# Hybrid encoder layer: the sums of w_out are prepared in the first chunk instead of the second, the parts of the first products move beside P, and the second chunk's conv is drained one unit later

## The chip, the cores and the metric

The kernel runs on one core of a Trainium2 chip. The metric is the device time of one execution in microseconds (us); the times of a kernel are given as the median of several runs.

## The reference, cut to what matters

One encoder layer over 18 blocks of 128 tokens (two of a prompt, sixteen of a sample) and 16 learned meta tokens. One projection feeds a windowed attention with 8 query and 2 key heads and a depthwise convolution of width 31; both are gated, joined and projected out.

```python
h = rmsnorm(z, norm_w)
q, k, v, g_att, c_val, c_glu, g_conv = split(h @ w_in)
q, k = rmsnorm(q, q_norm_w), rmsnorm(k, k_norm_w)          # per head, 64 wide
att = windowed_gqa(q, k, v, sink) * silu(g_att)            # 128 back, 128 ahead, meta keys, sink
u = c_val * sigmoid(c_glu)
y = depthwise_conv(u, conv_w) + conv_b                     # 31 taps
cnv = silu(layernorm(y, ln_w, ln_b)) * silu(g_conv)
out = z + concat(att, cnv) @ w_out
```

## The kernel before, in words

All products are in fp32r, each operand split in a high part and the rest of it, and each product made in three passes (high by high, high by low, low by high). A tile's high part is a cast on ScalarE (ACT), its low part a subtraction on VectorE (DVE).

**Projection.** The tokens form six groups (group 0 has 400 columns with the meta tokens, the others 384), three of them a chunk. For each chunk the units of w_in (256 columns each) are run through in a fixed order: the four conv units U_C (value and glu of 128 channels), the conv gates U_GC, the attention gates U_GA, k and v (U_KV), and the two query units U_Q. A product of a unit with a group or a block of 128 tokens is a tile pj in PSUM, 24 matmuls (8 slices of the model width in three passes). There are four such tiles, so a product has to wait until the product four ahead of it was read. L1028 is the product whose result has tokens in rows (q, k, v), L1012 the other. For q the reader is DVE: L1159 multiplies pj by rqq, the inverse root mean square that GpSimd (POOL) makes from ACT's squares (L177, L178). For k and v they are L1186 and L1178, and L1196 to L1199 transpose and scale k.

**Conv.** It runs on DVE, 31 taps for each of four channel groups and each chunk (L1086 for the first tap, L1095 for the other 30), on 1167 columns at once. The taps wait in a queue conv_q; each part of the program that has other work calls tick with the time that TensorE (PE) will spend on it, and tick issues taps for so much time. owe takes off the time of other DVE work. A loop "while conv_q: tick(3000)" stands ahead of one unit of each chunk and issues all taps that are left.

**LayerNorm of the conv.** For each block of 128 tokens, ln_block issues three steps, a tick apart: s1 transposes the four channel groups (lnt, PE, L250) and takes the statistics (DVE L253, L254, then POOL for the inverse root and the scaled mean); s2 applies them (zn, DVE L263); s3 transposes back (lnu, PE, L269), ACT makes the silu (L272) and the result is stored. One block is begun in a tick, from LN_WAIT ticks on after the chunk's last tap was issued.

**Attention and the output.** Attention begins inside the second chunk's last query unit: spread is called there after each product and begins the slots of attention, n counting the calls. After the projection attention_rest runs the other slots, with PE and POOL in program order. slot_step issues what is due in a slot t: acts (loads, gates, splits), the scores S of a block, and jobs, the output products. Two blocks b0 = 2p and b1 = 2p + 1 make a pair p. The first two 128-row slices of each half of w_out are multiplied in a form with seven products of sums instead of eight; their names are c1, s3, s2, s1, t0, t1, s4, and JOBS gives each the slot, counted from 16 p, in which product (L719, tile yb) issues it. An operand of activations lies in HOME, the place of a tile rest in which parts finds the high and the low half; two_parts (L677, L678) fills it. rest takes the space of the projection's weights, so it exists from attention_rest on, and with_rest puts off what needs it.

**The sums.** The seven operands of w_out, for two slices i, are made on the chip: presplit_sums loads four pieces of w_out (wor) and then takes one step a tick: 14 operands in all get a cast (ACT, L392, tiles woc, wot, wos) and a subtraction (DVE, L393) and a store of 512 KB to wod in DRAM; between them stand 8 differences of pieces (DVE, L397). An operand lies in one of the two buffers of the tag xn, which the row statistics of the input use also; the pieces take the four buffers of the tag xt, which the loads of x use. In split_at presplit_sums(0) is called behind the second group of the second chunk's second conv unit and presplit_sums(1) behind the last group of its third.

PIECES_W lists the 22 pieces of wod in the order in which they are wanted. The first APART go to tiles of their own, the next to slots of wo, loaded by load_wo, and the last ones to rest.

Inside the manual parts the order of PE or POOL is the program's. Elsewhere a scheduler that models the engines picks the order of each engine's instructions from what the program has issued, so moving work on one engine moves others' too.

Of the kernel before, what the change touches and what calls it, by code (L numbers as in the profile page):

```python
# [18 lines left out]
P = 128  # L19
# [28 lines left out]
W0 = 3  # L48
LN_WAIT = (9, 2)
LTAGS = "dbdbd" + "dcdcddddd"  # L50
# [31 lines left out]
NS = 2  # L82
PIECES_W = [("c1", 0), ("c1", 1), ("s3", 0), ("s3", 1), ("s2", 0), ("s2", 1), (6, 0), (6, 1), (7, 0), (7, 1)]
PIECES_W += [("s1", 0), ("s1", 1), ("t0", 0), ("t0", 1), (2, 0), (2, 1), (3, 0), (3, 1)]
PIECES_W += [("s4", 0), ("s4", 1), ("t1", 0), ("t1", 1)]
APART = 3
JOBS = (
# [21 lines left out]
SUMS = ("c1", "s3", "s2", "s1", "t0", "t1", "s4")  # L109
HOME = {"c1": 0, "t1": 0, "s3": 1, ("c", 0): 1, "s4": 1, "s1": 2, "s2": 3, ("c", 1): 3, "t0": 4, ("t", 0): 5, ("t", 1): 5}  # L110
QP = 7
# [4 lines left out]
U_C = [0, 1, 2, 3]  # L116
# [12 lines left out]
def hymba_kernel(  # L129
# [287 lines left out]
    def load_apart(i):  # L417
        if i < 2:
            t = pool["b"].tile([P, D], F32R, tag=f"wa{i}", name=f"wa{i}", bufs=1)
        else:  # L420
            t = cst["pt" if i < APART else "rest"][:, 6:8].rearrange("p a n -> p (a n)")
        wo[PIECES_W[i]] = t
        nc.sync.dma_start(t.bitcast(F32), wod[i])
# [247 lines left out]
    def parts(name):  # L671
        t = cst["rest"][:, HOME[name]].rearrange("p (h e n) -> p h e n", h=2, n=P)
        return t[:, 0], t[:, 1]
# [77 lines left out]
    for p in range(NB // 2):  # L751
        b0, b1 = 2 * p, 2 * p + 1
        for rel, f in (
            (5, lambda b0=b0: load_mix(b0)),
            (6, lambda b1=b1: load_mix(b1)),
            (9, lambda p=p: load_x(p, (0, 1))),
            (11, lambda b1=b1: mix_conv(b1)),
            (12, lambda b0=b0: mix_conv(b0)),
            (13, lambda p=p: with_rest(lambda: mix_diff(p))),
            (12, lambda p=p: load_x(p, (1, 1))),  # L760
            (13, lambda b1=b1: with_rest(lambda: two_parts("c1", cnt[b1][:, 0:NS, :]))),
            (14, lambda: with_rest(lambda: two_parts("s3", temp(0)))),
            (17, lambda b0=b0: two_parts(("c", 0), cnt[b0][:, NS:4, :])),
            (17, lambda p=p: load_x(p, (0, 0))),
            (20, lambda b1=b1: two_parts(("c", 1), cnt[b1][:, NS:4, :])),
            (18, lambda p=p: load_x(p, (1, 0))),
            (18, lambda p=p: add_kept(p, (1, 1), 0)),
            (20, lambda p=p: add_kept(p, (0, 0), 1)),
            (21, lambda p=p: add_kept(p, (1, 0), 0)),
        ):  # L770
            acts.setdefault(16 * p + rel, []).append(f)
        for rel, name, es in JOBS:
            to = late_jobs if name == "s3" else jobs
            if p == LAST and name in ("t1", (1, 0)):
                for c0 in (0, 256):
                    to.setdefault(16 * p + rel, []).append((p, name, es, c0, 256))
            else:
                to.setdefault(16 * p + rel, []).append((p, name, es))
# [32 lines left out]
    def spread(b):  # L811
# [6 lines left out]
        if n == 9:  # L818
            mixing_open()
        if n in (10, 11, 12):  # L820
            load_apart(n - 10)
# [10 lines left out]
    def attention_rest():  # L832
# [6 lines left out]
        for k in range(6):  # L839
            later(2 + k, lambda k=k: load_wo(12 + k))  # L840
        later(9, lambda: load_apart(len(PIECES_W) - 1))
        while slots:
# [7 lines left out]
    if True:  # L850
# [483 lines left out]
        for n3 in range(3):  # L1334
# [8 lines left out]
            (1, U_C[0], CHUNKS[1][2]): lambda: presplit_wo(3),  # L1343
            (1, U_C[1], CHUNKS[1][1]): lambda: presplit_sums(0),
            (1, U_C[2], CHUNKS[1][2]): lambda: presplit_sums(1),
        }

        for i, (c, u, g) in enumerate(items):
            if (c, u) == (1, U_KV) and g == CHUNKS[c][0]:
                while conv_q[0] or conv_q[1]:  # L1350
                    tick(3000)
# [118 lines left out]
```

## Time and profile before

| | |
|---|---|
| median of 3 runs | 950.04 us (948.38 to 951.31) |
| the profiled execution | 948.39 us |
| its span, first to last instruction | 946.6 us |
| mean granted TensorE clock | 0.996 |

The profile is of one execution. Its parts: busy time of each engine; what each engine waited for; a timeline of its instructions with the wait ahead of each in brackets and what ended it; and windows, which give for a stretch the busy time of each engine (with its number of instructions in brackets), the mean granted clock of TensorE, the share of time that the DMA engines were busy, and GB/s. In every row names lose their numbers (lnu for lnu8), and L is the line of the kernel. A busy figure alone says little here: an engine that is late matters only when PE waits for it.

### The profile page before, as it was taken

The numbers are of one execution on the slowest core, as the hardware profiler recorded it, in microseconds if no ns is written. First come the engines' busy times: TensorE is split into PE (matmuls) and PEld (weight loads), VectorE is DVE, ScalarE is ACT, GpSimd is POOL, SyncE is SP. The second block draws the span as 40 slices with busy tenths as digits, with TensorE's granted clock in tenths as the row PEclk, the third lists the DMA queues.
The fourth block names the chain that finished last, engine by engine and source line by source line (L and its number), as shares of the span: only waits on it lengthen the run. The fifth ranks groups of instructions, "written<-read, shape, count | busy, mean of one in ns | idle before, by whom it ended". The sixth has DMA issues, their size and how long they took to land. (4 is left out here: it accounts for less than half of the span.)

```text
span 946.6 us, 16874 instructions
## 1 busy us (share of the span) xinstructions
PE 929.8 (98%) x5734; PEld 878.8 (93%) x5734; DVE 778.6 (82%) x1340; ACT 445.5 (47%) x1229; POOL 358.9 (38%) x553
## 2 busy tenths in 40 slices
PE   8999999999999999999999889999999999999998
PEld 8999999999999999999999889887888888888887
DVE  5579999997977889999996763688888888897884
ACT  7432022253458742011111354567676776776772
POOL 4310000282558300000001452677665465546644
PEclk9999999999999999999999999999999999999999
DMA  8584345685756587333333468997565665665421
GB/s 304 169 273 194 134 176 179 247 294 189 207 169 194 185 285 260 147 114 140 131 139 133 143 194 272 376 374 210 166 181 170 185 197 153 186 199 168 144 92 48
DMA packets 146342, 182.80 MB, mean 193 GB/s; under 512 B 40944, under 2 KB 106816, under 8 KB 146128
## 3 DMA queue, kind: packets, MB, share of 16 engines
q1 hardware_dynamic: 146256, 181.72, 58.7%
q8 instruction: 45, 0.74, 0.3%
q14 instruction: 41, 0.34, 0.1%
HBM read 115.83 MB, written 65.85 MB: 192 GB/s over the span
## 5 line engine op out<-in xcount | busy, mean ns | idle before, releaser
L1012 PE MATMUL pj<-xh,ws 128*128 128x384 f32 (+1 forms) x1536 | 395.9, 338 | 0.1
L1095 DVE SCALAR_TENSOR_TENSOR y<-us,cw,y 128x1167 f32<-128x1167 f32 x240 | 329.3, 1431 | 0.1
L1012 PEld LDWEIGHTS pj<-xh,ws 128*128 128x128 f32 x1536 | 280.1, 188 | 0.4 <-ACT xh L1260 0.4
L1012 PE MATMUL pj<-xl,ws 128*128 128x384 f32 (+1 forms) x768 | 260.9, 340 | 0.1
L719 PE MATMUL yb<-wo,rest 128*128 128x512 f32 (+1 forms) x717 | 190.8, 399 | 0.0
L1028 PE MATMUL pj<-ws,xh 128*128 128x256 f32 (+1 forms) x880 | 165.2, 285 | 0.2 <-DVE kn L1186 0.2
L719 PEld LDWEIGHTS yb<-wo,rest 128*128 128x128 f32 x717 | 125.9, 189 | 22.6 <-DVE rest L678 0.2
L1012 PEld LDWEIGHTS pj<-xl,ws 128*128 128x128 f32 x768 | 144.1, 188 | 0.5 <-DVE xl L950 0.4
L1028 PEld LDWEIGHTS pj<-ws,xh 128*128 128x128 f32 (+1 forms) x880 | 137.5, 188 | 1.1 <-issue 0.4
L1028 PE MATMUL pj<-ws,xl 128*128 128x256 f32 (+1 forms) x440 | 124.6, 283 | 0.0
L1120 ACT ACTIVATE go<-pj 128x384 f32<-128x384 f32 x48 | 23.5, 490 | 154.2 <-PE pj L1012 140.3
L534 ACT ACTIVATE sb<-sb,nm 128x304 f32<-128x304 f32 (+5 forms) x144 | 77.8, 541 | 32.4 <-DVE nm L522 30.4
L177 POOL TENSOR_SCALAR ssk<-ssk 128x2 f32<-128x2 f32 x18 | 10.5, 582 | 209.1 <-ACT sqk L1134 208.9
L522 DVE CUSTOM_DVE_ANT_0 sb<-S,bias,vec 128x304 f32<-128x304 f32 (+5 forms) x144 | 74.1, 515 | 16.7 <-PE S L464 15.8
L560 POOL TENSOR_SCALAR sb<-sb,es 128x304 f32<-128x304 f32 (+5 forms) x144 | 73.2, 526 | 38.3 <-PE pT_x L580 17.0
L1028 PEld LDWEIGHTS pj<-ws,xl 128*128 128x128 f32 (+1 forms) x440 | 83.0, 189 | 0.2
L177 POOL TENSOR_SCALAR ssq<-ssq 128x4 f32<-128x4 f32 (+2 forms) x55 | 27.0, 491 | 109.5 <-ACT xn L875 70.4
L464 PE MATMUL S<-kw,q 128*128 128x304 f32 (+5 forms) x288 | 63.3, 302 | 0.6 <-issue 0.5
L464 PEld LDWEIGHTS S<-kw,q 128*128 128x128 f32 x288 | 52.5, 188 | 11.2 <-ACT keptFalse L737 0.8
L642 POOL TENSOR_TENSOR at<-at,ga 128x256 f32<-128x256 f32 x36 | 26.7, 742 | 75.1 <-DVE at L636 75.1
L730 DVE TENSOR_TENSOR yo<-yb,yo 128x512 f32<-128x512 f32 (+1 forms) x55 | 37.1, 674 | 15.3 <-PE yb L719 15.1
L988 DVE TENSOR_TENSOR ws<-wraw,ws 128x512 fp32r<-128x512 f32 x50 | 34.8, 727 | 8.2 <-ACT ws L987 8.2
(156 smaller groups left out, 1368.0 us busy)
## 6 DMA issues: line engine op xcount, KB each, us to landing
wd<-ws SPq DMA_DIRECT2D x36, 512.0 KB, 5.9
ws<-wd SPq DMA_DIRECT2D x36, 512.0 KB, 5.9
wraw<-in_w_in SPq DMA_DIRECT2D x52, 256.0 KB, 5.8
xn<-in_z SPq DMA_DIRECT2D x18, 512.0 KB, 5.4
gd<-go SPq DMA_DIRECT2D x48, 192.0 KB, 1.9
yo<-in_z SPq DMA_DIRECT2D x36, 256.0 KB, 3.7
wo<-wod SPq DMA_DIRECT2D x18, 512.0 KB, 7.5
out_y<-yo SPq DMA_DIRECT2D x35, 256.0 KB, 2.4
```

The costliest lines, as they stand in the source:

```text
L177: nc.gpsimd.tensor_scalar(src, src, scale, eps, op0=ALU.mult, op1=ALU.add)
L464: r = f(*a, **k)
L522: nc.vector.tensor_tensor_reduce(out=sb[:, n, c0:c1], in0=ps[:, 0:w], in1=cst["bias"][:, kv, at + c0 : at + c1], scale=1.0, scalar=nsnk[:, ...
L534: nc.scalar.activation(sb[:, n, c0:c1], sb[:, n, c0:c1], AF.Exp, bias=nm[:, n : n + 1], scale=-1.0, accum_out=rs[:, n : n + 1],)
L560: nc.gpsimd.tensor_scalar(sb[:, k, a0:a1], sb[:, k, a0:a1], es[:, k : k + 1], 1.0, op0=ALU.mult, op1=ALU.mult)
L642: nc.gpsimd.tensor_tensor(at[:, pr, :], at[:, pr, :], gat[b][:, pr, :], op=ALU.mult)
L719: nc.tensor.matmul(ps[:, :n], x[mi][:, i, :], w[wi], start=((name, e) in OPENS and k == 0), stop=(done and e == es[-1] and k == 2), skip_g ...
L730: nc.vector.tensor_tensor(y, ps[:, :n], y, op=ALU.add)
L988: pinned(eng.tensor_tensor(lo, raw[q], hi, op=ALU.subtract), k < 2)
L1012: nc.tensor.matmul(ps[:, :n], ws[:, d, wi, P * half_i : P * half_i + P], x[xi][:, d, o : o + n], start=(k == 0), stop=(k == 3 * ND - 1),)
L1028: nc.tensor.matmul(ps[:rows, :UW], x[xi][:, d, o : o + rows], ws[:, d, wi, :], start=(k == 0), stop=(k == 3 * ND - 1),)
L1095: nc.vector.scalar_tensor_tensor(y[:, yo + o0 : yo + o1], u[:, o0 + k : o1 + k], cw[:, j, k : k + 1], y[:, yo + o0 : yo + o1], op0=ALU.mul ...
```

## The change

It has six parts.

1. presplit_sums(0) and (1) are called behind the last group of the first chunk's first attention-gate unit and behind the first group of its U_KV.
2. The loop that drains conv_q stands ahead of U_Q[0] (keys[-2]) instead of ahead of U_KV in the second chunk, and LN_WAIT of that chunk is 1 instead of 2.
3. The parts move: c1 and t1 share slot 6 and s3, ("c", 0) and s4 slot 7 of the tile pt (called ptiles in the profile), which exists before rest does; the others take four places of rest instead of six. c1's split no longer waits for rest.
4. APART is 2: the pieces 2 to 19 lie one slot of wo later each, and the last two in rest.
5. In each pair b1's conv rows and gates are loaded before b0's.
6. In pair 0, c1's split is at step 12 and its product at step 14, one earlier than in the other pairs.

```diff
-LN_WAIT = (9, 2)
+LN_WAIT = (9, 1)
...
-APART = 3
+APART = 2
...
-HOME = {"c1": 0, "t1": 0, "s3": 1, ("c", 0): 1, "s4": 1, "s1": 2, "s2": 3, ("c", 1): 3, "t0": 4, ("t", 0): 5, ("t", 1): 5}
+HOME = {"c1": ("pt", 6), "t1": ("pt", 6), "s3": ("pt", 7), ("c", 0): ("pt", 7), "s4": ("pt", 7)}
+HOME.update({"s1": ("rest", 0), "s2": ("rest", 1), ("c", 1): ("rest", 1), "t0": ("rest", 2)})
+HOME.update({("t", 0): ("rest", 3), ("t", 1): ("rest", 3)})
...
     def load_apart(i):
-        if i < 2:
+        if i < APART:
             t = pool["b"].tile([P, D], F32R, tag=f"wa{i}", name=f"wa{i}", bufs=1)
         else:
-            t = cst["pt" if i < APART else "rest"][:, 6:8].rearrange("p a n -> p (a n)")
+            k = 2 * (i - len(PIECES_W) + 4)
+            t = cst["rest"][:, k : k + 2].rearrange("p a n -> p (a n)")
...
-            (5, lambda b0=b0: load_mix(b0)),
-            (6, lambda b1=b1: load_mix(b1)),
+            (5, lambda b1=b1: load_mix(b1)),
+            (6, lambda b0=b0: load_mix(b0)),
...
-            (13, lambda b1=b1: with_rest(lambda: two_parts("c1", cnt[b1][:, 0:NS, :]))),
+            (13 - (p == 0), lambda b1=b1: two_parts("c1", cnt[b1][:, 0:NS, :])),
...
         for rel, name, es in JOBS:
             to = late_jobs if name == "s3" else jobs
+            rel -= p == 0 and name == "c1"
...
-            (1, U_C[1], CHUNKS[1][1]): lambda: presplit_sums(0),
-            (1, U_C[2], CHUNKS[1][2]): lambda: presplit_sums(1),
+            (0, U_GA[0], CHUNKS[0][2]): lambda: presplit_sums(0),
+            (0, U_KV, CHUNKS[0][0]): lambda: presplit_sums(1),
         }
 
         for i, (c, u, g) in enumerate(items):
-            if (c, u) == (1, U_KV) and g == CHUNKS[c][0]:
+            if (c, u) == keys[-2] and g == CHUNKS[c][0]:
                 while conv_q[0] or conv_q[1]:
                     tick(3000)
```

The instructions of PE, DVE and ACT keep their number and kind; their order moves at three places. In the rows, names carry their numbers, lines of the changed kernel are up to six higher than those before, and "x4" is four in a row.

The first is PE near the end of the second chunk's k and v. lnt8 and lnu8 are the two transposes of block 8's LayerNorm, zn8 is what DVE makes between them, pj133 the last product of U_KV and pj134 the first of U_Q[0]. Before:

```order
L1028 MATMUL pj133_5633<-ws1_8_4949,xh5_3484 128x256
L269 MATMUL lnu8_5345<-ident_72,zn8_5287 128x128 x4
L250 MATMUL lnt10_5393<-ident_72,y1_0_3769 128x128
L250 MATMUL lnt10_5393<-ident_72,y1_1_3974 128x128
L250 MATMUL lnt10_5393<-ident_72,y1_2_4327 128x128
L250 MATMUL lnt10_5393<-ident_72,y1_3_4724 128x128
L1196 MATMUL kt12_5409<-ident_72,kn12_5324 128x128
L250 MATMUL lnt11_5462<-ident_72,y1_0_3769 128x128
L250 MATMUL lnt11_5462<-ident_72,y1_1_3974 128x128
L250 MATMUL lnt11_5462<-ident_72,y1_2_4327 128x128
L250 MATMUL lnt11_5462<-ident_72,y1_3_4724 128x128
L269 MATMUL lnu9_5414<-ident_72,zn9_5355 128x128 x4
```

The same place in the changed kernel:

```order
L271 MATMUL lnu8_5525<-ident_72,zn8_5467 128x128 x4
L1034 MATMUL pj133_5537<-ws1_8_4949,xh5_3564 128x256
L1034 MATMUL pj133_5537<-ws1_8_4949,xl5_3565 128x256
L1034 MATMUL pj133_5537<-ws1_8_4949,xh5_3564 128x256 x2
L1034 MATMUL pj133_5537<-ws1_8_4949,xl5_3565 128x256
L1034 MATMUL pj133_5537<-ws1_8_4949,xh5_3564 128x256
L252 MATMUL lnt10_5573<-ident_72,y1_0_3849 128x128
L252 MATMUL lnt10_5573<-ident_72,y1_1_4043 128x128
L252 MATMUL lnt10_5573<-ident_72,y1_2_4346 128x128
L252 MATMUL lnt10_5573<-ident_72,y1_3_4724 128x128
L1034 MATMUL pj134_5611<-ws1_6_5140,xh3_3116 128x256
L1034 MATMUL pj134_5611<-ws1_6_5140,xl3_3117 128x256
```

Before, lnu8 stood at the end of pj133, 15 of its matmuls behind the last transpose of lnt8, and lnu9 behind it with only transposes between. In the changed order lnt8 stands whole behind pj131 and lnu8 18 matmuls into pj133; lnt9 stands behind pj132, lnu9 in pj134, and the later blocks follow one about every product: from lnt8 to lnu8 there are 42 projection matmuls, from lnt9 to lnu9 47, then 48 for block 10, 40 for block 11 and 61 for block 12. lnu17, the last, stands behind pj141.

The second place is DVE in the first chunk's first query unit. y0_2 and y0_3 are the conv's taps, qs0_2 reads the product pj61, and wor and wos belong to the sums. Before:

```order
L1095 SCALAR_TENSOR_TENSOR y0_2_1350<-us0_2_740,cw_80,y0_2_1350 128x1167
L1159 TENSOR_TENSOR qs0_1_2597<-pj60_2561,rqq0_1_2590 128x256
L1095 SCALAR_TENSOR_TENSOR y0_3_1524<-us0_3_956,cw_80,y0_3_1524 128x1167
L1159 TENSOR_TENSOR qs0_2_2638<-pj61_2599,rqq0_2_2630 128x256
L1095 SCALAR_TENSOR_TENSOR y0_2_1350<-us0_2_740,cw_80,y0_2_1350 128x1167
L1199 SCALAR_TENSOR_TENSOR ks7_2503<-kt7_2501,kscale_81,ks7_2503 128x128
L1095 SCALAR_TENSOR_TENSOR y0_3_1524<-us0_3_956,cw_80,y0_3_1524 128x1167
```

The changed kernel:

```order
L1101 SCALAR_TENSOR_TENSOR y0_2_1350<-us0_2_740,cw_80,y0_2_1350 128x1167
L399 TENSOR_TENSOR wor22_1_2264<-wor22_1_2264,wor11_1_2258 128x2x256
L1101 SCALAR_TENSOR_TENSOR y0_3_1524<-us0_3_956,cw_80,y0_3_1524 128x1167
L1165 TENSOR_TENSOR qs0_1_2676<-pj60_2636,rqq0_1_2665 128x256
L1101 SCALAR_TENSOR_TENSOR y0_2_1350<-us0_2_740,cw_80,y0_2_1350 128x1167
L399 TENSOR_TENSOR wor21_1_2260<-wor21_1_2260,wor22_1_2264 128x2x256
L1101 SCALAR_TENSOR_TENSOR y0_3_1524<-us0_3_956,cw_80,y0_3_1524 128x1167
L395 TENSOR_TENSOR wos3_1_2563<-wor12_1_2262,wos3_1_2563 128x512
L1101 SCALAR_TENSOR_TENSOR y0_2_1350<-us0_2_740,cw_80,y0_2_1350 128x1167
L395 TENSOR_TENSOR wos2_1_2622<-wor22_1_2264,wos2_1_2622 128x512
L1165 TENSOR_TENSOR qs0_2_2718<-pj61_2678,rqq0_2_2709 128x256
L1205 SCALAR_TENSOR_TENSOR ks7_2574<-kt7_2572,kscale_81,ks7_2574 128x128
```

Of the 22 operations of the sums five stand ahead of the first L988 of unit 6 in the changed order, sixteen between it and qs0_2, and one behind qs0_3; qs0_2 has two taps more ahead of it than before and eight row scalings of x (L921) less. The first and the last of the 22 are 96 rows apart; before it was 53. The second chunk's DVE order is without them, and its last tap stands ahead of ks9.

The third place is PE where the projection ends (pj151 is its last product) and the output products yb begin. S2_0_0 are the scores of block 2, which need q2_2, the transposed and split copy of what qT2 makes. Before:

```order
L1028 MATMUL pj151_6625<-ws1_7_5702,xh5_3484 128x256
L719 MATMUL yb0_6743<-wa0_6235,rest_6707 128x512 x3
L719 MATMUL yb0_6743<-wa1_6289,rest_6707 128x512 x3
L464 MATMUL S1_1_3_6751<-kw1_5950,q2_1_6352 128x176 x2
L580 MATMUL pT1_c_0_6768<-ident_72,sb2_5966 128x128 x4
L464 MATMUL S2_0_0_6776<-kw0_5949,q2_2_6725 128x176 x2
L719 MATMUL yb0_6743<-ptiles_6186,rest_6707 128x512 x3
L719 MATMUL yb0_6743<-wo0_6363,rest_6707 128x512 x3
L614 MATMUL O0_1_6691<-ptiles_6186,vm_78 128x512
```

The changed kernel:

```order
L1034 MATMUL pj151_6624<-ws1_7_5606,xh5_3564 128x256
L723 MATMUL yb0_6716<-wa0_6235,ptiles_6186 128x512 x3
L723 MATMUL yb0_6716<-wa1_6289,ptiles_6186 128x512 x3
L467 MATMUL S1_1_2_6724<-kw1_5868,q2_1_6351 128x208 x2
L467 MATMUL qT2_6727<-ident_72,q2_6443 128x128 x4
L467 MATMUL S1_1_3_6752<-kw1_5868,q2_1_6351 128x176 x2
L583 MATMUL pT1_c_0_6767<-ident_72,sb2_5884 128x128 x4
L467 MATMUL S2_0_0_6775<-kw0_5867,q2_2_6732 128x176 x2
L723 MATMUL yb0_6716<-wo0_6362,ptiles_6186 128x512 x6
```

yb0's first six matmuls take their operand from ptiles instead of rest. S1_1_2 and qT2, which stood ahead of pj151 before, now stand behind these six, and between qT2 and S2_0_0 there are only S1_1_3 and pT1_c_0.

More of the change, by code (lines that the diff above doesn't have):

```diff
@@ L671, in parts @@
     def parts(name):
-        t = cst["rest"][:, HOME[name]].rearrange("p (h e n) -> p h e n", h=2, n=P)
+        place, k = HOME[name]
+        t = cst[place][:, k].rearrange("p (h e n) -> p h e n", h=2, n=P)
         return t[:, 0], t[:, 1]
@@ L819, in spread @@
             mixing_open()
-        if n in (10, 11, 12):
+        if n in (10, 11):
             load_apart(n - 10)
@@ L840, in attention_rest @@
             later(2 + k, lambda k=k: load_wo(12 + k))
-        later(9, lambda: load_apart(len(PIECES_W) - 1))
+        for k in range(2):
+            later(8 + k, lambda k=k: load_apart(len(PIECES_W) - 2 + k))
         while slots:
```

## The prediction

> **What bounds the kernel now.** I read the page first. TensorE (PE) is busy all but all of the span, so only what makes PE wait, or run at a lower clock, can move the time; time taken off another engine counts where PE waits for it.
>
> ```profile
> span 946.6 us, 16874 instructions
> PE 929.8 (98%) x5734; PEld 878.8 (93%) x5734; DVE 778.6 (82%) x1340; ACT 445.5 (47%) x1229; POOL 358.9 (38%) x553
> ```
>
> Next the list of PE's waits (us in total, times, longest). It names all that is to be had near the change: the conv's LayerNorm (lnu and lnt behind zn) and one wait of an output product for its operand (yb behind rest).
>
> ```profile
> PE lnu L269 <- DVE zn L263: 6.2, 2, 3.4
> PE O L614 <- DVE ptiles L597: 1.6, 1, 1.6
> PE yb L719 <- ACT rest L677: 1.0, 1, 1.0
> PE lnt L250 <- DVE zn L263: 0.5, 1, 0.5
> ```
>
> The timeline puts them at places (start, duration, wait in brackets), and the windows show the granted clock around the two long ones (the last four columns are POOL, PEclk, DMA share and GB/s).
>
> ```profile
> 540.62 0.66 PE L269 MATMUL lnu<-ident,zn 128*128 128x128 f32 x4 [2.79 <-DVE zn L263]
> 568.49 1.06 PE L269 MATMUL lnu<-ident,zn 128*128 128x128 f32 x4 [3.39 <-DVE zn L263]
> 614.87 0.50 PE L614 MATMUL O<-ptiles,vc 128*128 128x512 f32 x1 [1.65 <-DVE ptiles L597]
> 620.50 1.69 PE L719 MATMUL yb<-wa,rest 128*128 128x512 f32 x6 [1.04 <-ACT rest L677]
> 538.00:546.00 8.00, 5.38 (x33) 5.24 (x34) 4.74 (x10) 4.08 (x14) 4.42 (x12) 0.79 0.85 300
> 566.00:574.00 8.00, 5.51 (x34) 5.54 (x35) 1.62 (x2) 3.11 (x10) 2.09 (x8) 0.79 0.90 308
> 610.00:620.00 10.00, 7.77 (x57) 6.68 (x55) 7.92 (x20) 6.96 (x21) 8.60 (x16) 1.00 1.02 349
> ```
>
> So the second chunk's LayerNorm costs 2.79 + 3.39 + 0.5 (lnt, in the list) of idle time, and 0.21 x 8 = 1.68 us of lost clock behind each long gap: 6.7 + 3.4 = **10.1 us**. The 1.65 us gap at 614.87 left the clock at 1.00.
>
> **LayerNorm of the second chunk: -10.1, with 1.0 left.** The gaps come from order: PE's program has lnu8 in pj133, some 15 products behind the last transpose of lnt8, and little other work ahead of lnu9. This is how the chain ran where PE waited longest (two blocks' statistics together, then POOL's scale, then zn):
>
> ```profile
> 563.83 1.30 DVE L253 BATCH_NORM_STATS2 bs<-lnt 128x6 f32<-128x512 f32 x2 [0.23 <-PE lnt L250]
> 567.54 0.81 DVE L263 TENSOR_SCALAR zn<-lnt,mv 128x512 f32<-128x512 f32 x1 [1.83 <-POOL mv L256]
> ```
>
> From 563.83 to lnu at 568.49 it is 4.7 us. A projection matmul takes 2.82/24 = 0.118 us (rows at 266.76 and 267.11 below: 0.35 for three). In the changed order lnt8 to lnu8 has 42 of them between (4.9 us), lnt9 to lnu9 47 (5.5), lnt10 to lnu10 48 (5.7), lnt11 to lnu11 40 (4.7), lnt12 to lnu12 61 (7.2). All cover 4.7, the shortest just so. I take the whole 10.1 back, less 1.0 for short waits at the shortest ones (an estimate: two of 0.5, like lnt's). The new order needs the conv done earlier, since lnt8 stands whole behind pj131. The last taps were issued here:
>
> ```profile
> 530.50 2.90 DVE L1095 SCALAR_TENSOR_TENSOR y<-us,cw,y 128x1167 f32<-128x1167 f32 x2
> 329.42 0.69 DVE L393 TENSOR_TENSOR woc<-wor,woc 128x512 fp32r<-128x512 f32 x1 [1.06 <-ACT woc L392]
> 336.68 0.69 DVE L393 TENSOR_TENSOR wot<-wor,wot 128x512 fp32r<-128x512 f32 x1 [3.62 <-ACT wot L392]
> 337.76 0.68 DVE L397 TENSOR_TENSOR wor<-wor,wor 128x512 f32<-128x512 f32 x1
> 338.36 0.88 DVE L1086 TENSOR_SCALAR y<-us,cw,vec 128x1167 f32<-128x1167 f32 x1
> 357.33 0.69 DVE L393 TENSOR_TENSOR wot<-wor,wot 128x512 fp32r<-128x512 f32 x1 [2.06 <-ACT wot L392]
> ```
>
> The sums leave that stretch: 14 L393 and 8 L397, each 0.60 start to start (337.76 to 338.36), 13.2 us, and DVE's waits for their casts, 1.06 + 3.62 + 2.06 = 6.7. VectorE (DVE) is then some 20 us less behind, and the taps, which ended at 533.4, end near 513 and what the first chunk loses. pj131 ends 48 products ahead of the wait at 540.62 - 2.79 = 537.8, near 532: over 14 us of cover.
>
> **The sums in the first chunk: +3.1, and 0.9 for their own waits.** DVE has little room there. From 219.95 to the last tap's end it is idle 56.15 - 52.42 = 3.7 us; just ahead of it is a wait of 4.07.
>
> ```profile
> 219.95:276.10 56.15, 55.90 (x472) 55.25 (x470) 52.42 (x80) 24.00 (x128) 28.93 (x40) 1.00 0.64 200
> 219.95 1.29 DVE L988 TENSOR_TENSOR ws<-wraw,ws 128x512 fp32r<-128x512 f32 x2 [4.07 <-ACT ws L987]
> 230.48 2.19 DVE L921 SCALAR_TENSOR_TENSOR xt<-xt,vec,bc 128x384 f32<-128x384 f32 x4 [0.67 <-PE bc L904]
> 262.81 0.42 DVE L1159 TENSOR_TENSOR qs<-pj,rqq 128x256 f32<-128x256 f32 x1
> 269.56 0.42 DVE L1159 TENSOR_TENSOR qs<-pj,rqq 128x256 f32<-128x256 f32 x1 [1.19 <-POOL rqq L178]
> 274.73 1.42 DVE L1095 SCALAR_TENSOR_TENSOR y<-us,cw,y 128x1167 f32<-128x1167 f32 x1
> 276.07 0.42 DVE L1159 TENSOR_TENSOR qs<-pj,rqq 128x256 f32<-128x256 f32 x1
> 266.76 0.28 PE L1028 MATMUL pj<-ws,xl 128*128 128x256 f32 x1
> 267.11 0.29 PE L1028 MATMUL pj<-ws,xl 128*128 128x256 f32 x1
> 283.66 0.38 PE L250 MATMUL lnt<-ident,y 128*128 128x128 f32 x2
> ```
>
> Five of the 22 operations stand ahead of 219.95 in the new order and fall into the 4.07. Sixteen of the others stand ahead of qs0_2, which empties pj61 for pj65, and two taps more (1.34 each, 274.73 to 276.07), less eight row scalings (L921, 2.19 for four with the last one's tail, so 0.53 each): 9.6 + 2.7 - 4.2 = 8.1, of which 2.4 fall into the waits that lie ahead of qs0_2 in the trace. So qs0_2 moves from 262.81 to 268.5 and ends at 268.9. PE wants pj65 at 283.66 - 6 x 2.82 = 266.7: a wait of 2.2. The same walk for the next two gives 0.4 and 0.5 more (pj66, pj67): **3.1**. The last tap then ends at 286.5, and the transposes behind pj70, at 283.66 + 3.1 = 286.8, find it done.
>
> That walk has DVE without a gap. Its bounds: 0 more, and 6.7 more if its waits for casts come along (the three rows above). I take 0.9, nearer the lower end: the 22 operations stand among 96 rows of DVE's order instead of 53, so each cast has more time, and DVE comes to qs later than before, when POOL's factors are long done. PE would wait for DVE one for one.
>
> [...]
>
> **The start of the output products: +1.3.** c1's parts no longer wait for rest, and yb's 1.04 goes. But S1_1_2 and qT2, which were ahead of pj151, now stand behind it, and S2_0_0 follows them closely. The chain from qT to its copy, at the next such place:
>
> ```profile
> 637.79 0.60 PE L464 MATMUL qT<-ident,q 128*128 128x128 f32 x4
> 638.15 0.71 PE L614 MATMUL O<-ptiles,vm 128*128 128x512 f32 x2
> 638.43 0.58 ACT L484 CAST q<-qT 64x512 fp32r<-64x512 f32 x1 [0.71 <-PE qT L464]
> 640.34 0.69 DVE L487 TENSOR_TENSOR q<-qT,q 64x512 fp32r<-64x512 f32 x1
> 622.03 0.36 PE L464 MATMUL S<-kw,q 128*128 128x176 f32 x2
> 622.58 0.44 PE L464 MATMUL S<-kw,q 128*128 128x176 f32 x2
> ```
>
> qT leaves PE at 638.15, and the copy is whole at 640.34 + 0.69 = 641.03: 2.9 us. Between qT2 and S2_0_0 there is only 622.58 - 622.03 = 0.55 of PE work (S1_1_3, pT1_c_0). PE waits 2.3 there, where it waited 1.04: **+1.3**; behind the waiting S2_0_0 stand yb's next six and O0_1 on the same engine, in program order. The 1.65 at 614.87 stays. Costed at nothing: the other storage of parts and the piece count 3 to 2 (PE never waited for wo's pieces; each has a slot one later, in a DMA that is full, 1.02 in the window from 610), and load_mix's order (two loads of one size). Their cover gone would show as a wait of yb for wo.
>
> **Sum.** -10.1 + 1.0 + 3.1 + 0.9 + 1.3 = -3.8. The profiled execution took 948.39 (span 946.6 and 1.8 around it), so 944.6; the runs' median is 950.04, 1.65 above, so **946.3**.
>
> **The rivals.** (The measurement can tell 0.3%, 2.9 us: faster is below 947.2, slower above 952.9.)
>
> A, my forecast, 946.3, with 944 to 949 by its bounds: chance 0.42, of it 0.28 faster and 0.14 the same.
>
> B, the first chunk hides the sums: DVE fills its waits better than my walk, or pj's four tiles cover it. Without 3.1 + 0.9 the time is 942.3. For it: PE waited for nothing there before. Against: 3.7 us of idle time cannot hold 10.2 us of work (17 x 0.60). Chance 0.23, faster.
>
> C, the other side: ScalarE (ACT) takes its casts in order, and a cast waits until the store of the operand two ahead has left its buffer; ACT's work for k and q queues behind it, and DVE waits as at 336.68 and 357.33. With the 6.7 of those rows in full, and one gap then over 2.79 (1.7 of clock): -10.1 + 1.0 + 3.1 + 6.7 + 1.7 + 1.3 = +3.7, so 953.7. It decides from where DVE's extra waits pass 3.0 (no gain left), and is measurably slower from 5.9. For it: the rows. Against: the casts' slower pace, and that stretch's stores share DMA that is 0.64 busy. Chance 0.13.
>
> D, the last LayerNorm gap stays: the last block has no later block to stand between, and 3.39 + 1.7 come back instead of the 1.0: -3.8 + 4.1 = +0.3, so 950.3. For it: one gap was at the end in this trace. Against: lnu17 now has some eight products behind it to come. Chance 0.16: 0.13 the same, 0.03 slower.
>
> E, POOL is starved. One small POOL operation ran thus beside seven taps without a break, and its like after them:
>
> ```profile
> 183.75 9.62 POOL L177 TENSOR_SCALAR ssq<-ssq 128x1 f32<-128x1 f32 x1 [63.63 <-ACT xn L875]
> 183.82 9.50 DVE L1095 SCALAR_TENSOR_TENSOR y<-us,cw,y 128x1167 f32<-128x1167 f32 x7
> 194.09 0.19 POOL L177 TENSOR_SCALAR ssq<-ssq 128x1 f32<-128x1 f32 x1
> ```
>
> If DVE, now without gaps, does this to one of the factors that qs waits for, qs is late by 9.4, and PE with it: -3.8 + 9.4 + 1.7 = +7.3, so 957.3. Against: taps in that stretch are broken up by reads of pj, and the longest wait for rqq was 1.19. Chance 0.06, slower. [...]
>
> **The numbers.** Faster 0.28 + 0.23 = 0.51; the same 0.14 + 0.13 = 0.27; slower 0.13 + 0.03 + 0.06 = 0.22. The range goes from 941 (B with no wait left over, 942.3 - 1.0) to 954 (C); outside are E and the tails, under 2 in 10. A alone has 944 to 949.
>
> **What would show it.** Right: no wait of lnu for zn over 1 us and the granted clock 1.00 from 535 to 580; waits of pj (L1028 in this kernel) for qs of about 3 us in all near 265 to 275; a wait of S for q near 622 of about 2.3, and none of yb for rest. Wrong: no wait of pj there (B); DVE waiting for wot, wos or woc in the first chunk for over 3 us (C); a long lnu wait near 570 with the clock below 1.00 (D); a POOL row of several us with qs behind it (E); a wait of yb for a wo piece, which none of the cases has.

## The result, and the profile after

| | before | changed |
|---|---|---|
| median of 15 runs each | 950.18 us (947.60 to 952.14) | 953.12 us (949.05 to 956.83) |
| the profiled execution's span | 946.6 us | 950.3 us |
| mean granted clock in it | 0.996 | 0.992 |

The changed kernel is slower by 0.3%: the ratio of the runs is 1.003, with a 95% interval of 1.0016 to 1.0045. The forecast was 946.3, faster.

The page's first lines and the list of PE's waits for the changed kernel (in us: total, times, longest):

```profile
span 950.3 us, 16878 instructions
PE 933.4 (98%) x5734; PEld 882.8 (93%) x5734; DVE 779.3 (82%) x1340; ACT 443.8 (47%) x1229; POOL 362.7 (38%) x553
...
PE pj L1034 <- DVE kn L1192: 6.5, 1, 6.5
PE S L467 <- ACT ptiles L599: 2.2, 1, 2.2
PE O L617 <- DVE ptiles L600: 1.4, 1, 1.4
...
PE lnu L271 <- DVE zn L265: 0.5, 1, 0.5
```

PE's idle time is what it was: 950.3 - 933.4 = 16.9 us, before 946.6 - 929.8 = 16.8. The 6.7 us of the second chunk's LayerNorm are gone, and a wait of 6.5 in the first chunk stands in their place. What the span grew by is busy time, and that is clock: 0.008 x 950.3 = 7.6 us lost to it, before 0.004 x 946.6 = 3.8. The windows show where (the last four columns are POOL, PEclk, DMA share, GB/s):

```profile
240.00:260.00 20.00, 15.38 (x131) 15.18 (x129) 19.01 (x33) 10.56 (x44) 10.00 (x11) 1.00 0.87 283
260.00:280.00 20.00, 18.07 (x135) 18.10 (x136) 18.55 (x28) 8.13 (x45) 10.03 (x12) 0.83 0.97 332
...
520.00:540.00 20.00, 20.00 (x168) 20.00 (x167) 7.95 (x18) 6.44 (x35) 4.95 (x11) 1.00 0.63 191
540.00:560.00 20.00, 20.00 (x175) 20.00 (x174) 11.60 (x30) 9.41 (x36) 9.47 (x24) 1.00 0.80 239
560.00:580.00 20.00, 20.00 (x175) 20.00 (x173) 11.18 (x32) 10.00 (x29) 9.58 (x25) 1.00 0.89 292
...
610.00:620.00 10.00, 8.51 (x50) 7.52 (x50) 6.57 (x17) 5.32 (x18) 8.18 (x15) 0.83 0.99 335
620.00:630.00 10.00, 7.76 (x37) 6.38 (x36) 7.75 (x21) 7.13 (x21) 2.97 (x6) 0.83 1.05 385
```

From 520 to 580, where PE had been idle for 6.7 us with a clock of 0.91 in two windows, it is busy without a break at 1.00. The losses are at 240 to 280 and at 610 to 630.

**The first chunk.** PE's wait, and VectorE's rows that lead to it:

```profile
261.93 0.55 PE L1034 MATMUL pj<-ws,xh 128*128 128x256 f32 x1 [6.55 <-DVE kn L1192]
```

```profile
219.38 0.69 DVE L395 TENSOR_TENSOR wos<-wor,wos 128x512 fp32r<-128x512 f32 x1 [1.49 <-ACT wos L394]
...
221.34 1.29 DVE L994 TENSOR_TENSOR ws<-wraw,ws 128x512 fp32r<-128x512 f32 x2
...
229.22 0.28 DVE L1192 TENSOR_TENSOR kn-1_2106<-pj,rqk-1_2100 16x128 f32<-16x128 f32 x1 [1.31 <-POOL rqk-1_2100 L180]
...
231.44 0.29 DVE L1192 TENSOR_TENSOR kn<-pj,rqk 128x128 f32<-128x128 f32 x1 [0.40 <-POOL rqk L180]
...
252.85 0.29 DVE L1184 TENSOR_TENSOR vs<-pj,vs 128x128 fp32r<-128x128 f32 x1 [0.99 <-ACT vs L1183]
253.06 1.43 DVE L1101 SCALAR_TENSOR_TENSOR y<-us,cw,y 128x1167 f32<-128x1167 f32 x1
254.40 1.89 DVE L994 TENSOR_TENSOR ws<-wraw,ws 128x512 fp32r<-128x512 f32 x3
256.21 1.43 DVE L1101 SCALAR_TENSOR_TENSOR y<-us,cw,y 128x1167 f32<-128x1167 f32 x1
257.55 0.68 DVE L994 TENSOR_TENSOR ws<-wraw,ws 128x512 fp32r<-128x512 f32 x1
258.15 0.68 DVE L399 TENSOR_TENSOR wor<-wor,wor 128x512 f32<-128x512 f32 x1
258.76 0.68 DVE L395 TENSOR_TENSOR wos<-wor,wos 128x512 fp32r<-128x512 f32 x1
259.36 0.28 DVE L1184 TENSOR_TENSOR vs<-pj,vs 128x128 fp32r<-128x128 f32 x1
259.56 0.68 DVE L395 TENSOR_TENSOR wos<-wor,wos 128x512 fp32r<-128x512 f32 x1
260.16 1.42 DVE L1101 SCALAR_TENSOR_TENSOR y<-us,cw,y 128x1167 f32<-128x1167 f32 x1
261.50 0.48 DVE L1192 TENSOR_TENSOR kn<-pj,rqk 128x128 f32<-128x128 f32 x2
```

The last two kn of U_KV are read from pj at 261.5. PE has been standing since 255.4, four products further on, with no tile free. From 252.85 on VectorE has no gap at all: three taps, four splits of ws and three operations of the sums stand ahead of kn in its fixed order. Behind the gap the clock was half for 4.8 us of PE's work, to 266.7 (0.50 to 0.57 in the windows of 2 us from 261 to 267), 2.4 us more. ScalarE's hold for a store did come, but behind kn, and PE did not wait for it:

```profile
269.96 0.62 ACT L394 CAST wos<-wor 128x512 fp32r<-128x512 f32 x1 [11.56 <-DMA wod<-wos]
```

The 1.31 for rqk-1, the factor of the meta tokens' kn, has a cause of its own. The sums' operands use the two buffers xn of the input's row statistics, and the load of the last x for these was issued at 216.9, before the change at 202.3 (with the sums back it is at 202.2 again; where the sums alone moved, at 215.6, with a wait of 1.30). So POOL makes that last statistic just when the first factors of k are wanted:

```profile
223.44 1.79 POOL L179 TENSOR_SCALAR ssq<-ssq 128x1 f32<-128x1 f32 x1 [13.37 <-ACT xn L881]
225.31 2.83 POOL L180 TENSOR_TENSOR rstd<-ssq,half 128x1 f32<-128x1 f32 x1
```

**The start of the output products.** Two waits of PE, and the windows of 2 us around them:

```profile
614.21 0.50 PE L617 MATMUL O<-ptiles,vc 128*128 128x512 f32 x1 [1.41 <-DVE ptiles L600]
...
624.59 0.43 PE L467 MATMUL S<-kw,q 128*128 128x176 f32 x2 [2.24 <-ACT ptiles L599]
```

```profile
614.00:616.00 2.00, 1.79 (x8) 1.53 (x8) 1.95 (x6) 1.91 (x8) 1.11 (x3) 0.72 1.01 352
616.00:618.00 2.00, 2.00 (x11) 2.00 (x11) 1.19 (x3) 0.32 (x2) 2.00 (x6) 0.50 0.98 369
618.00:620.00 2.00, 2.00 (x16) 1.91 (x16) 0.00 (x0) 0.29 (x2) 1.06 (x2) 0.92 0.93 284
...
624.00:626.00 2.00, 1.41 (x6) 1.21 (x7) 1.94 (x7) 1.46 (x5) 0.00 (x0) 0.78 1.12 378
626.00:628.00 2.00, 2.00 (x7) 1.50 (x6) 1.01 (x4) 1.05 (x4) 0.00 (x0) 0.50 1.02 399
628.00:630.00 2.00, 2.00 (x11) 1.74 (x10) 1.94 (x5) 1.12 (x3) 0.00 (x0) 0.86 1.01 402
```

The wait of S for its copy is 2.24 us, about the 2.3 that was worked out. But each of the two waits was followed by 3.41 us at half the clock (0.50 from 614.89 to 618.30 and from 625.13 to 628.54), 1.7 us of PE's time each, and the wait of O, 1.65 before and 1.41 now, had cost no clock before (1.00 from 610 to 620).

### The profile page after: what moved, and what is told of

It reads as the page before. It is cut to its first block, busy times and chain, and to the rows that moved or that the text cites. A ratio compares the mean times of both kernels' runs of the same rounds, so it can differ in the third digit from the quotient of the medians.

```text
span 950.3 us, 16878 instructions
## 1 busy us (share of the span) xinstructions
PE 933.4 (98%) x5734; PEld 882.8 (93%) x5734; DVE 779.3 (82%) x1340; ACT 443.8 (47%) x1229; POOL 362.7 (38%) x553
## 4 chain that ended last, share of the span: by engine, by line
PE 91%; DVE 3%; POOL 3%; DMA 2%; issue 1%; ACT 1%; SPq 0%; DVEq 0%; POOLq 0%
PE pj L1018 41%; PE yb L723 19%; PE pj L1034 14%; PE O L617 5%; PE S L467 4%; PE pT_m L583 2%; PE pT_c L583 1%; PE pT_x L583 1%; PE warmup L1251 1%; PE lnu L271 1%; PE lnt L252 1%; DVE xt L927 1%; PE qT L467 1%; DMA wraw<-in_w_in 1%; POOL xl L956 1%
## 5 line engine op out<-in xcount | busy, mean ns | idle before, releaser
L1034 PE MATMUL pj<-ws,xh 128*128 128x256 f32 (+1 forms) x880 | 167.2, 287 | 6.5 <-DVE kn L1192 6.5
L723 PE MATMUL yb<-wo,rest 128*128 128x512 f32 (+1 forms) x498 | 132.2, 399 | 0.0
L723 PEld LDWEIGHTS yb<-wo,rest 128*128 128x128 f32 x498 | 87.0, 189 | 15.3
L179 POOL TENSOR_SCALAR ssk<-ssk 128x2 f32<-128x2 f32 x18 | 7.6, 424 | 207.2 <-ACT sqk L1140 206.9
L723 PE MATMUL yb<-wo,ptiles 128*128 128x512 f32 x216 | 60.8, 411 | 0.0
L1061 ACT ACTIVATE sg<-pj 128x384 f32<-128x384 f32 (+1 forms) x24 | 11.8, 492 | 97.6 <-PE pj L1018 88.7
```

The costliest lines, as they stand in the source:

```text
L179: nc.gpsimd.tensor_scalar(src, src, scale, eps, op0=ALU.mult, op1=ALU.add)
L723: nc.tensor.matmul(ps[:, :n], x[mi][:, i, :], w[wi], start=((name, e) in OPENS and k == 0), stop=(done and e == es[-1] and k == 2), skip_g ...
L1034: nc.tensor.matmul(ps[:rows, :UW], x[xi][:, d, o : o + rows], ws[:, d, wi, :], start=(k == 0), stop=(k == 3 * ND - 1),)
```

## The experiments

All times are medians; a kernel's ratio is to the kernel before on the same chips, with its 95% interval. The kernel before stood at 950.2 to 950.3 throughout.

### Parts of the change undone

**The sums back in the second chunk**, all else as changed:

```diff
-            (0, U_GA[0], CHUNKS[0][2]): lambda: presplit_sums(0),
-            (0, U_KV, CHUNKS[0][0]): lambda: presplit_sums(1),
+            (1, U_C[1], CHUNKS[1][1]): lambda: presplit_sums(0),
+            (1, U_C[2], CHUNKS[1][2]): lambda: presplit_sums(1),
```

> The changed kernel with the sums of w_out prepared in the second chunk again, as before; all else as changed. Theory: the changed kernel's time against before is the sum of three places: the first chunk's k and v (+10: a wait of 6.5 us of pj for kn, and some 3.4 us at a lower clock behind it), the second chunk's LayerNorm (-10) and the start of the output products (+4: waits of S and O, and the clock behind them). The first goes here, and the LayerNorm's gain stays, because the later drain and LN_WAIT alone put enough products between lnt and lnu: about 944, and no wait of pj for kn over 1 us. Rival: the LayerNorm's gain hangs on DVE being rid of the sums in the second chunk; then its two long gaps return with their slow clock and the time is about 954.

Measured: 944.76 us, ratio 0.9942 (0.9923 to 0.9961). The theory's number. PE's wait for kn is 0.3, before 0.2, and the LayerNorm keeps 2.0 of waits in three pieces, with the clock at 1.00 from 520 to 600. Moving the sums costs 953.12 - 944.76 = 8.4 us, and the LayerNorm's gain does not need it.

**The drain and LN_WAIT back**, the sums early:

```diff
-LN_WAIT = (9, 1)
+LN_WAIT = (9, 2)
...
-            if (c, u) == keys[-2] and g == CHUNKS[c][0]:
+            if (c, u) == (1, U_KV) and g == CHUNKS[c][0]:
```

> The changed kernel with the second chunk's conv drained ahead of U_KV again and LN_WAIT 2 again; the sums stay in the first chunk. Theory: the first chunk's loss does not depend on these, and the order has 40 rows between lnt8 and lnu8 as before the edit, so the LayerNorm shows no gap either: about 953, as the changed kernel. Rival: the LayerNorm's gain comes from the drain and LN_WAIT alone; then its gaps are back, and the time is about 963 (953 + 10).

Measured: 958.27 us, 1.0085 (1.0061 to 1.0109). Between the two: with the sums early the drain and LN_WAIT are worth 958.3 - 953.1 = 5.2 us. The profiled execution had the wait for kn (5.7), other waits at the start of the output products (2.4 of pT_c for POOL, 2.3 of O), and two lnu waits, 2.4 in the second chunk and one in the first:

```profile
305.04 0.66 PE L271 MATMUL lnu<-ident,zn 128*128 128x128 f32 x4 [1.96 <-DVE zn L265]
```

So early sums also take away most of the second chunk's gaps, but can open one in the first chunk's LayerNorm. The profiled execution of the changed kernel has 0.5 there; three more kernels with early sums, below, have this same 1.96 (c1 at 15, the sums alone, nine matmuls), and two of them (the sums alone, nine matmuls) and this one lost some 1.7 us of clock there (0.91 from 300 to 320).

**c1 of pair 0 at the step of the others:**

```diff
-            (13 - (p == 0), lambda b1=b1: two_parts("c1", cnt[b1][:, 0:NS, :])),
+            (13, lambda b1=b1: two_parts("c1", cnt[b1][:, 0:NS, :])),
...
-            rel -= p == 0 and name == "c1"
```

> The changed kernel with c1's split at step 13 and its product at step 15 for pair 0 too, as for the other pairs. Theory: S1_1_2 and qT2 stand ahead of pj151 again, S2_0_0 finds its copy, the 2.2 us wait near 624 and the slow clock behind it go, and c1's parts are still not tied to rest: about 3 to 4 us less than the changed kernel, 949 to 950. Rival: what is lost there comes from the parts' place beside P or from c1's cast on ScalarE, not from the step; then the time stays at 953 and another wait stands near 622.

Measured: 951.49 us, 1.0017 (1.0000 to 1.0034), 1.6 us less than the changed kernel, where 3 to 4 were expected. The wait of S near 624 went; two new ones of yb for the parts in ptiles came, 1.1 and 0.9. The 1.6 is small beside the spread of the runs (8.5 us here), and this trace's wait for kn was shorter too (4.8, with 1.7 of slow clock less: 0.91 from 260 to 280, where the changed kernel has 0.83), which the step does not touch.

**Both, the sums back and c1 at 15:**

> Both edits: the sums in the second chunk as before, and c1 of pair 0 at step 15. Theory: what is left of the change is the LayerNorm's gain (-10) and the yb wait of 1.0 that goes: 939 to 941, faster than both kernels. Rival (the gain hangs on the sums): about 950.

Measured: 942.69 us, 0.9922 (0.9903 to 0.9941): faster than both kernels as the theory has it, 1.7 above its range. Beside 944.76 the step costs 2.1 us, so with the other pair of kernels 1.6 to 2.1.

**The drain and LN_WAIT alone**, on the kernel before:

> The kernel before with only the second chunk's drain ahead of U_Q[0] and LN_WAIT 1. Theory: this alone makes the LayerNorm's gain, and the parts' places, the piece count and the order of the loads are worth no more than the yb wait of 1.0: 941 to 944, beside 942.7 with these too. Rival: the places of the parts are needed for the gain (less work in front of the attention): 947 or more.

Measured: 940.80 us (940.61 to 941.31), 0.9902 (0.9885 to 0.9919): the fastest of all, and faster than with the other parts of the change. Its PE rows and the windows of the second chunk's LayerNorm:

```profile
557.49 0.63 PE L269 MATMUL lnu<-ident,zn 128*128 128x128 f32 x4 [1.23 <-DVE zn L263]
558.96 0.63 PE L269 MATMUL lnu<-ident,zn 128*128 128x128 f32 x4 [0.40 <-DVE zn L263]
```

```profile
540.00:560.00 20.00, 18.37 (x158) 17.98 (x157) 12.69 (x36) 10.03 (x29) 11.65 (x31) 1.00 0.86 271
560.00:580.00 20.00, 19.46 (x167) 19.11 (x166) 8.58 (x17) 10.61 (x31) 7.49 (x17) 1.00 0.84 267
```

Some short waits are left (1.0 of yb for rest among them), none of them with a lower clock (1.00 in every window looked at). Its 6 runs are also closer together (0.7 us) than the 15 of before (4.5) and of the changed kernel (7.8).

**The order of the loads, on top of that:**

```diff
-            (5, lambda b0=b0: load_mix(b0)),
-            (6, lambda b1=b1: load_mix(b1)),
+            (5, lambda b1=b1: load_mix(b1)),
+            (6, lambda b0=b0: load_mix(b0)),
```

> The kernel with the drain and LN_WAIT alone (940.8), and the loads of b1 ahead of those of b0. With the parts' places and the piece count on top it was 942.7. If the order of the loads is what costs the 1.9, it is 942 to 943 here; if it is the places, 940.5 to 941.3.

Measured: 941.07 us, 0.9896 (0.9879 to 0.9913). The order of the loads costs nothing that can be told; the places of the parts and the piece count, with c1's split no longer put off until rest exists, are all that 942.69 has besides, and cost 1.6.

**The sums alone moved**, on the kernel before:

> The kernel before with only the sums moved to the first chunk. From the kernels so far (the sums cost 8.4 when all else is changed; the changed order shows no long lnu wait even with the old drain): about 950 minus some 8 of the LayerNorm plus some 10 of the first chunk, 951 to 955, with the pj wait for kn near 255. Rival: without the later drain the LayerNorm's gaps stay, and it is 958 or more.

Measured: 954.53 us, 1.0041 (1.0027 to 1.0056), the time that was expected, 4.3 more than before. The wait for kn was 4.9. Of lnu a wait of 2.9 was left in the second chunk, and the 1.96 in the first chunk was there.

**The split of c1 one step earlier**, on the kernel of 942.69:

```diff
-            (13, lambda b1=b1: two_parts("c1", cnt[b1][:, 0:NS, :])),
+            (12, lambda b1=b1: two_parts("c1", cnt[b1][:, 0:NS, :])),
```

> The kernel with the sums back and c1 of pair 0 at step 15 (942.7, with a wait of 1.1 us of yb for ptiles), in which every pair's split of c1 is one step earlier, 12, and the products stay at 15. Theory: the split was all that yb waited for, so that wait goes and nothing takes its place: about 941.5. Rival: in the other pairs ScalarE's cast one step earlier stands ahead of work that the scores wait for, 9 times some 0.4 us: 943 to 946.

Measured: 942.44 us, 0.9922 (0.9906 to 0.9938): no difference, neither theory. The wait of yb for ptiles stayed at 1.1. It stands at 639 in the trace of 942.69, behind a part made from temp (`DVE L682 ptiles<-temp`, 638.49), and c1's is made from cn; so c1's split was not what it waited for.

### What makes kn late

**The casts and stores without VectorE's work:**

```diff
-            nc.vector.tensor_tensor(lo, raw[key], hi, op=ALU.subtract)
+            nc.scalar.copy(lo, raw[key])
...
-            nc.vector.tensor_tensor(raw[dst], raw[x], raw[y], op=ALU.subtract)
+            pass
```

> The changed kernel with the sums' loads, casts and stores in the first chunk, but without their 22 operations on VectorE: the 8 differences are left out, and the low halves are a second cast on ScalarE, so the output products use other numbers than w_out's sums. Theory: VectorE's queue is what makes kn late, so the wait of pj for kn shrinks from 6.5 to under 2 us and the clock stays up: 944 to 947. Rival: the casts and the stores that hold ScalarE in order are the cause, and 14 casts more make it worse: a wait of 6 us or more stays, 953 or more.

Measured: 955.63 us, 1.0055 (1.0037 to 1.0073). Against the theory: the one long wait went, but PE waited as much in pieces, and ScalarE stood for stores of k as well as of the sums (this trace is of an execution of 952.28, below the median):

```profile
PE pj L1034 <- DVE kn L1192: 3.4, 2, 2.1
...
PE kt L1202 <- DVE kn L1192: 2.0, 1, 2.0
PE pj L1034 <- ACT ws L993: 1.9, 1, 1.9
...
ACT ks L1204 <- DMA kd<-ks: 6.1, 4, 2.5
...
ACT wos L394 <- DMA wod<-wot: 3.0, 2, 1.6
ACT wos L394 <- DMA wod<-wos: 2.7, 3, 1.6
```

VectorE's 13.2 us are thus not the whole of it. But this kernel gives ScalarE 14 more casts, so it does not say that its load alone is nothing. The next two add one thing each to the kernel of 940.80.

**The traffic alone:**

```diff
+    def copies_only(b):
+        for k in range(3):
+            nc.sync.dma_start(spare[b, k], vd[b - 1 : b + 1])
...
             later(1, fin)
+            if 1 <= b < 8:
+                later(3, lambda: copies_only(b))
```

> The kernel with the drain and LN_WAIT alone (940.8), and in the first chunk's k and v stretch 21 copies of 256 KB from vd to unused DRAM, 10.8 MB read and written, as much as the sums' loads (4) and stores (7) there; no cast and no VectorE work is added. Theory 1 (VectorE's queue makes kn late): the time stays at 940 to 943. Theory 2 (the traffic makes the stores of k and v land late, ScalarE waits for their buffers in order, and kn and PE with it): waits of ScalarE for vd and kd of several us, a wait of pj for kn of 3 us or more, 946 or more.

Measured: 948.87 us, 0.9975 (0.9960 to 0.9989), 8.1 us more than 940.80. The theory of the traffic, in time; but the wait for kn was 1.3 and not 3, ScalarE had no waits for vd, and PE's longest wait (2.9, in a stretch with a clock of 0.92 from 260 to 280) was for a qs near 276. ScalarE waited for the stores of k 19.2 us in all:

```profile
PE pj L1033 <- DVE qs L1164: 3.6, 2, 2.9
...
PE pj L1033 <- DVE kn L1191: 1.3, 1, 1.3
...
ACT ks L1203 <- DMA kd<-ks: 19.2, 7, 5.5
```

The traffic is like that of the sums, not equal to it: 21 copies of 256 KB are 5.5 MB, 11 read and written, issued from 233 to 264; the sums' 8 loads of 256 KB and 14 stores of 512 KB are 9.4 MB, and most of their stores went out from 209 to 280.

**VectorE's load alone:**

```diff
+    def load_only(rk):
+        a, b = cst["idle"][:, 0], cst["idle"][:, 1]
+        for _ in range(2):
+            nc.vector.scalar_tensor_tensor(a, b, rk[:, 0:1], b, op0=ALU.mult, op1=ALU.subtract)
...
                 later(1, fin2)
+                if 0 <= b < 7:
+                    load_only(rk)
```

> The kernel with the drain and LN_WAIT alone (940.8), and 14 VectorE operations of the size of the sums' (two behind each of seven kn), on a tile of their own: no load, cast or store is added. Theory 1 (VectorE's queue): kn of the last blocks comes late behind them, a wait of pj for kn of 3 us or more in one piece near 255 with a lower clock behind it, 946 or more. Theory 2 (traffic and ScalarE): VectorE has the room, 941 to 943.

Measured: 955.63 us, 1.0048 (1.0031 to 1.0066), 14.8 more than 940.80. The theory of the queue in time, and more than that. The scheduler, with these in the list, put the other work in another order too, and PE waited 7.05 us in one piece until 260.4, here for a kn that it was to transpose (kt), not for a free tile. Either load is enough by itself to make PE wait in this stretch (2.9 in one piece with the copies, 7.05 here); the sums bring both.

### What the short waits cost in clock

**Nine idle matmuls where S waits:**

```diff
         ps = psum.tile([P, 512], F32, tag="a", name=f"S{b}_{kv}_{n}")
+        if (b, kv, n) == (2, 0, 0):
+            for _ in range(9):
+                nc.tensor.matmul(ps[:, :P], ident, ident, start=True, stop=True)
```

> The changed kernel with 9 matmuls of ident by ident into the tile of S2_0_0 ahead of it, where PE waits 2.2 us (their result is overwritten). Theory: the wait itself stays, filled, but the clock does not fall behind it: no clock below 1.00 in 622 to 630, about 1.7 us less in the runs where it fell, 951 to 952. Rival: the slow clock there follows the 1.4 us wait ten us earlier, or PE's load in all, and not that gap: the clock is 0.83 in that window as before, and the time 953 or, if the 9 run over the wait, more.

Measured: 951.55 us, 1.0013 (1.0001 to 1.0026), 1.6 less than the changed kernel, and as the theory has it in the place:

```profile
623.96 2.17 PE L510 MATMUL S<-ident 128*128 128x128 f32 x18
626.37 0.43 PE L467 MATMUL S<-kw,q 128*128 128x176 f32 x2 [0.23 <-ACT ptiles L602]
```

```profile
624.00:626.00 2.00, 2.00 (x20) 1.94 (x18) 1.61 (x5) 1.94 (x6) 1.72 (x5) 1.00 1.12 358
...
628.00:630.00 2.00, 2.00 (x12) 1.65 (x12) 1.98 (x6) 1.81 (x5) 0.00 (x0) 1.00 1.03 414
```

The stretch still takes its 2.2 us, filled, and the clock is not lowered behind it. It was lowered behind the wait of O ten us earlier (0.50 from 618 to 620). This fits the theory, but one execution does not show it: the kernel without VectorE's work has the same two waits unfilled, 1.4 for O and 2.2 for S, and no lower clock behind either.

```profile
610.00:620.00 10.00, 8.52 (x64) 7.61 (x63) 7.03 (x20) 5.75 (x19) 8.87 (x17) 1.00 1.06 359
620.00:630.00 10.00, 7.76 (x49) 6.67 (x49) 7.54 (x22) 7.42 (x21) 5.05 (x11) 1.00 1.06 378
```

So these two waits can cost 1.7 us each in clock, and need not. That the nine matmuls save it rests on the 1.6 of the medians, and the intervals of the two kernels (1.0001 to 1.0026, 1.0016 to 1.0045) overlap.

## Why the prediction was wrong

The kernels give each term by a difference, taken one after the other: 940.80 - 950.25 = -9.5 for the drain and LN_WAIT; 944.76 - 940.80 = +4.0 for the other parts; 953.12 - 944.76 = +8.4 for the sums. That they add up to +2.9 follows from how they are taken, and the sizes belong to this order: put first, on the kernel before, the sums cost 4.3, since they also take away part of the LayerNorm's gaps, and behind them the drain is worth 5.2.

**The LayerNorm, forecast -10.1 + 1.0 = -9.1: right**, in mechanism and in size (-9.5). Only its source was laid to two edits where one is enough: both the later drain and the early sums spread the blocks, and the second adds little once the first is there. (Twice the forecast says products where its numbers count matmuls: the 15 between lnt8 and lnu8, and pj131's 48. The times worked out from them stand.)

**The sums in the first chunk, forecast 3.1 + 0.9 = 4.0: the step that failed**, measured 8.4. The walk of VectorE without a gap was sound as far as it went. It looked for the first late reader at qs0_2 and pj65, when the reader that is late first is kn7, four products earlier. From its first split of ws at 221.34 to kn at 261.50 VectorE worked 37.5 us and waited 2.7. By the walk without a gap kn7 is thus at 219.95 + 37.5 = 257.4, and PE wants the tile at 283.66 - 10 x 2.82 = 255.5, so the wait by load alone is the same 2 us or so, in another place. What was mis-sized is the term for VectorE's own waits, 0.9. From 219.95 to kn7 the trace has 221.34 - 219.95 = 1.4 (a late start, behind the 1.49 for a cast), 1.31, 0.40 and 0.99: 4.1 us, which is the whole way from 257.4 to 261.5. And the lower clock behind the wait, for which the forecast's sum had nothing, cost 2.4 more.

The reason given for the small value was that VectorE would come to its reads later than POOL's factors were done, so that waits would vanish. Up to 274 that holds for qs. It does not hold for the first kn of the stretch, whose factor stood behind the row statistic that the sums had put off, nor for a vs that hangs on ScalarE, which waited 1.79 for a store of v. The forecast weighed the sums' casts against the sums' own stores and left out that the stores of k and v, with few buffers each, land later too (medians of 3.3 and 3.8 us from issue to landing between 205 and 285, before 2.5 and 2.2). The run with copies alone shows that such traffic costs 8.1 us with no other work, though more at qs than at kn; the run with VectorE's load alone shows that added operations would have been enough as well. In the trace of the changed kernel the wait of 6.5 is some 2.0 of load, the 4.1, and 0.4 from kn's start until PE goes on; of the 4.1, 1.4 stand behind a cast, 1.7 behind POOL's factors and 1.0 behind a store of v. What would be left of the 8.4 with one of these taken away stays open.

**The start of the output products, forecast +1.3: mis-sized.** With its parts' places it is +4.0. The wait of S came as worked out (2.24 against 2.3), and yb's 1.04 went. Two sizes failed. The step of pair 0 with its wait costs 1.6 to 2.1, some of it clock in the executions where the clock falls: behind S the traced one lost 1.7 of clock (0.50 from 625.13 to 628.54), for which the forecast's sum had nothing. And the places of the parts and the piece count, costed at nothing, cost 1.6 where a gain of 1.04 was counted. In the kernel of 942.69 yb's 1.0 for rest is gone, but 1.1 of yb for ptiles and 0.8 of S for rest stand in its place; the rest was not traced.

**The rivals.** C gave the time, 953.7, mostly by another path. It had VectorE wait for the sums' casts, which it did for 2.8 us in the rows before 220 and no more than 0.6 after them: with 3.4 in all C's sign (over 3) was there, but of this only the late start of 1.4 reached kn. There C's mechanism was at work: the cast behind the 1.49 had itself stood 2.73 us for a store. The 11.56 us hold of ScalarE came too late to matter. That C's number was met is luck. B is out: nothing hid the sums. D is out: no gap was left at the end. E is out as a mechanism of its own: no POOL row of 9 us stands ahead of a late kn, though one of 2.83 stands ahead of the first.

## What to carry to other kernels

When work is moved into a stretch, walk the receiving engine's order to every reader that frees a tile for the critical engine, not only to the first that looks late, and keep the waits that the engine already has there in the walk. Count the moved work's transfers as well as its instructions: here 5.5 MB of copies alone, beside small stores with few buffers, cost 8.1 us. See also whose buffers the moved work takes: here it put off a row statistic, and that a factor of k. And try each part of a change by itself: here one part of six was worth 9.5 us, and the others gave back 12.3.

## What was not expected of the hardware

Waits of one length did and did not lower the clock. Behind the wait of O, 1.41 us in the changed kernel, 3.41 us ran at half the clock; behind 1.65 in the kernel before, 1.42 in the fastest one and 1.43 in the one without VectorE's work it stayed at 1.00, and that last one kept it behind 2.24 for S as well, where the changed kernel lost it behind the same 2.24. In the kernel with the sums alone moved, 2.89 of lnu at 577 left it at 1.00 too, where the kernel before lost it behind 2.79.

| kernel | the wait | granted clock behind it |
|---|---|---|
| before | lnu, 2.79 | 0.50 from 541.22 to 544.63 |
| before | lnu, 3.39 | 0.50 from 568.52 to 571.93 |
| before | O, 1.65 | 1.00 from 610 to 640 |
| changed | kn, 6.55 | 0.50 from 259.90, within the wait, to 266.73 |
| changed | O, 1.41 | 0.50 from 614.89 to 618.30 |
| changed | S, 2.24 | 0.50 from 625.13 to 628.54 |
| the drain and LN_WAIT alone | O, 1.42 | 1.00 from 605 to 640 |
| without VectorE's work | O, 1.43 | 1.00 from 615 to 640 |
| without VectorE's work | S, 2.24 | 1.00 from 625 to 640 |
| sums alone | lnu, 2.89 | 1.00 from 560 to 600 |

Between 20 us and the end the traces of before and changed have these five slow stretches and no other: four of 3.41 us and one, behind the longest wait, of 6.83. Behind the two shorter waits of the changed kernel that is 1.7 us of PE's time each; the waits of 1.65, 2.24 and 2.89 in the other kernels cost nothing in clock. By these rows the length of a wait does not settle it, and what does is not shown. Waits that cost clock in one execution and not in the next would make a kernel with several of them vary from run to run, and the runs are so (7.8 us apart, against 0.7 for the fastest kernel, whose clock is 1.00 in every window looked at); that the one makes the other is argued, not shown.
